# Gathered rows moved into earlier stages: four edits to a decoder block with a PEER layer

## The chip, the cores and the metric

The kernel runs on one core of one Trainium2 chip, as one launch. The metric is the device time of that launch in microseconds. Before the change it is 1765.07 us, the median of three runs (1763.4 to 1766.93).

## The reference, cut to what matters

One decoder block on 512 tokens of 1024 channels in float32. Two branches (retention and spatial gating) run on a normed input, are merged by gates and go through one output projection. Its result is scaled by a gate per channel and added to x:

```
x  = x + gate1 * (merged @ w_out)                    # residual
h2 = modulate(rms_norm(x, norm2_g), shift2, scale2)
q  = (h2 @ w_q) as (tokens, 8 heads, 2, 128);  s = q . sub_keys   # 128 scores per half
top 16 of each half;  cand = sub_s[0][:, None] + sub_s[1][None, :];  top 16 of the 256 sums
expert = k1 * 128 + k2                               # 16 of 16384 experts per head
act = gelu(h2 . expert_u[expert]) * softmax(top)     # 128 rows of 4 KB per token
x  = x + gate2 * sum(act * expert_v[expert]);  out = rms_norm(x, final_g)
```

So each token needs 128 rows of the table u and then 128 rows of the table v.

## The kernel before, in words

The 512 tokens are four tiles of 128. The last layer is done in two ways. For the first tile and the last one the rows are **gathered**: one indirect DMA from GpSimd's queue (line 934) brings one row for each of the 128 tokens, 0.524 MB, and one VectorE instruction takes it (`consume`): line 950 multiplies by h2 and sums to a dot, line 955 adds the row times its weight to `acc`. That is 4 x 128 = 512 gathers: u of the first tile (numbers 0 to 127), v of the first tile (128 to 255), then u and v of the last tile. For the two tiles between, all 16384 experts are computed as matmuls in 128 chunks, in a dense loop at the end (from line 1800): every chunk needs its v chunk, and its uT chunk has been done earlier (an `ahead` unit, plain f32, its result sent to `sd` and read back) or is done in the loop (`u_mm`, three passes).

The order is: modulation and the whole first tile (to some 290 us), including its lists of experts in four parts (`g_lists`, each raises `lim` by 32); 56 weight units for the other three tiles (`gemm`: w_in, w_sgu, w_ret); w_out, residual and second norm; query units; `ahead` units with lists and one-hots; the dense loop.

Weights come through a `Stream`: a unit of 512 KB lands in one of 5 `raw` buffers, ScalarE copies it to `wh` (line 87) and VectorE takes the rest `wl` (line 90), three units ahead of TensorE. A unit's optional `prep` runs on VectorE before that: the eight w_out units are multiplied by gate 1 there (line 344).

Gathers are set in program order. `gfree` is a list of free buffers, `gather_all` starts a gather for each while the number is under `lim`, `consume` takes the oldest and gives its buffer back. Behind each weight unit of the 56 `gemm` calls a hook, `bg_gather` (line 1017): it first works off one entry of `tq` (the first tile's remaining lists), then adds `GB1` to a credit (0.5 while `tq` is not empty) and takes as many rows as there is credit. Its buffers are two `ga`, one `gt` and one slot each of the rotating `wh` and `wl` tiles; before the two w_ret units two more `gt` are added, and after the first one `ga`, `wh` and `wl` are dropped. `lim` is 128 in this stage, and is set to 256 behind it (line 1230).

From the query units on, `plan` (line 103) writes the order out by hand. It keeps two clocks, P for TensorE and V for VectorE, and lets VectorE's steps in while V is at most P + 6. A credit pays for `gather` steps: `GPU` = 1.4 for each `ahead` unit, 1.0 for each query unit. What it holds up is drained behind the query units with more `ahead` units, so their number (NAH) comes out of it. What has not been gathered by then is spread evenly over the dense loop, on seven buffers.

The first tile's `acc0` lives in a pool opened behind the hooks (line 1228). `x2_tile` (line 1254) adds the w_out sums to x. Candidate sums of two lists are made by `stage2` on VectorE (lines 852 and 853), or earlier by `cands` on ScalarE (lines 840 and 841); the first tile uses the former.

Of the kernel before, what the change touches and what calls it, by code (L numbers as in the profile page):

```python
# [11 lines left out]
F32 = mybir.dt.float32  # L12
# [26 lines left out]
GPU = 1.4  # L39
GB1 = 2.2  # L40
VN = 2
# [61 lines left out]
def plan():  # L103
# [54 lines left out]
    for g in range(4):  # L158
        for u in range(4):
            if g and u:  # L160
                score(4 * (g - 1) + u)
            steps.append(("q", g, u))
            t["P"] += 4.2
            t["V"] += 1.15
            if t["go"]:
                t["credit"] += 1.0
            if g and not u:
                score(4 * (g - 1))
            pump()
# [21 lines left out]
def block_kernel(ctx: ExitStack, tc: tile.TileContext, a, out, dbg=None):  # L191
# [149 lines left out]
    for g in range(2):  # L341
        add_group(a["w_ret"], g)
    def gate_prep(r, g):
        V.tensor_tensor(r.rearrange("p (a n) -> p a n", a=2), r.rearrange("p (a n) -> p a n", a=2),
                        gates[:, 0:1, g * 512:(g + 1) * 512].to_broadcast([128, 2, 512]), op=OP.mult)
    add_two(a["w_out"], gate_prep)
    steps, NAH = plan()
# [630 lines left out]
    for g in range(4):  # L978
        units = []
        bks = [bank() for _ in range(4)]  # L980
        for u in range(4):
# [10 lines left out]
            if g and u == 2:  # L992
                st1_0(g - 1)
            if g == 2 and u == 3:
                stage2(l0, [(0, 0), (0, 1)])
# [8 lines left out]
        if g == 0:  # L1004
            h20_n()
    tq += [lambda: score0(3), lambda: st1_0(3), lambda: g_lists(l0, 0, GT[0], 1),
           lambda: stage2(l0, [(0, 4), (0, 5)]), lambda: g_lists(l0, 0, GT[0], 2),
           lambda: stage2(l0, [(0, 6), (0, 7)]), lambda: g_lists(l0, 0, GT[0], 3)]


    ga = [tmp.tile([128, 1024], F32, name="ga", tag="ada", bufs=4) for _ in range(2)]
    gfree += ga
    gfree.append(t0_tile("gt"))
    gfree += ["wh", "wl"]
    cr = [0.0]

# [194 lines left out]
    while any(dropped(b) for _, b in gt_t.values()):  # L1211
        consume()
        gather_all()
    bg[0] = lambda: None
    dump("mH", mH.bitcast(F32))
# [11 lines left out]
    h2F = hf.tile([128, ND, TA], F32, name="h2F")  # L1227
    GT[0].acc = kp.tile([128, D], F32, name="acc0")
    V.memset(GT[0].acc, 0.0)
    lim[0] = 2 * NJ  # L1230
    x2 = big([128, N3, D], F32, "x2")
# [8 lines left out]
    for u in range(4):  # L1240
        for g in range(2):
# [3 lines left out]
            if u < 2:  # L1245
                unit_mm("nat", u, w[0], w[1], mH, mL, [(bk[g][b], b) for b in range(N3)])
            else:
                last.append((u, g, w))
# [5 lines left out]
    def x2_tile(t):  # L1254
        for g in range(2):
            xx = x2[:, t, g * 512:(g + 1) * 512]
            V.tensor_tensor(xx, bk[g][t], xx, op=OP.add)
        P.dma_start(x2d[t + 1], x2[:, t, :])
# [655 lines left out]
```

## Time and profile before

| | us |
|---|---|
| median of three runs | 1765.07 |
| the profiled execution | 1765.71 |
| its span (first to last instruction) | 1763.7 |
| TensorE busy in it | 1589.2 (90%) |
| VectorE busy | 1414.4 (80%) |
| ScalarE busy | 581.4 (33%) |
| GpSimd busy | 750.5 (43%) |
| DMA, mean of the span | 341 GB/s, 601.82 MB |

PE is TensorE, PEld its weight loads, DVE is VectorE, ACT ScalarE, POOL GpSimd, SP the queue of plain loads. L955 is line 955 of the kernel. A row with `[1.20 <-DVE x L10]` says that the engine was idle for 1.20 us until line 10 on VectorE released it. "To landing" is the time from the issue of a DMA to its arrival. A gathered row of the first tile is named `E`, of the last one `EB`.

### The profile page before, as it was taken

To read this page: it belongs to the slowest core of one execution; us is meant where nothing else is said; L and a number is where in the kernel's file an instruction comes from. 1 tells how busy PE (TensorE), PEld (TensorE's weight loads), DVE (VectorE), ACT (ScalarE), POOL (GpSimd) and SP (SyncE) were. 2 spreads that over 40 slices of the span, in tenths; PEclk is the share of its full clock that TensorE was granted. 3 is DMA by queue.
4 is the path that set the end of the run, shared out by engine and by line. 5 is a ranking of instruction groups with operands and counts; after the bars stand their busy time and mean duration, and the time that the engine had idled before them with its cause. 6 is when DMAs were issued, how large, how long until landed. Compare 5 with 4: busy or idle time off the path is not lost.

```text
span 1763.7 us, 22139 instructions
## 1 busy us (share of the span) xinstructions
PE 1589.2 (90%) x7546; PEld 1237.1 (70%) x7546; DVE 1414.4 (80%) x2862; ACT 581.4 (33%) x914; POOL 750.5 (43%) x629
## 2 busy tenths in 40 slices
PE   9999999889999889999999998889888888888886
PEld 8544578789779768898888887556665656565553
DVE  7675356988789876999999994788878878888887
ACT  6322123332234234432136774242222222222222
POOL 0101001157447512146467653475545545555542
PEclk9999999989999889999999999899999999999998
DMA  8999857379879857479999999999999999999995
GB/s 334 381 353 377 320 193 261 124 270 373 287 246 351 307 187 280 156 258 410 387 391 375 389 390 366 373 407 409 408 408 408 408 408 408 408 408 406 408 405 207
DMA packets 168496, 601.82 MB, mean 341 GB/s; under 512 B 19072, under 2 KB 19072, under 8 KB 168256
## 3 DMA queue, kind: packets, MB, share of 16 engines
q0 software_dynamic: 87888, 320.64, 47.7%
q1 hardware_dynamic: 80496, 279.78, 42.1%
q8 instruction: 59, 0.97, 0.2%
q14 instruction: 53, 0.43, 0.1%
HBM read 568.89 MB, written 31.46 MB: 340 GB/s over the span
## 4 chain that ended last, share of the span: by engine, by line
DVE 25%; DMA 24%; PE 23%; issue 15%; POOL 9%; ACT 3%; SPq 0%; POOLq 0%; DVEq 0%; ACTq 0%
DMA gr<-in_v_dram,EB 10%; PE mm L416 6%; DVE acc L955 5%; POOL gr L934 4%; DMA gt<-in_v_dram,EB 3%; POOL gt L934 3%; DVE wl L90 3%; PE mm L384 2%; PE mm L385 2%; PE mm L383 2%; PE acc L1680 2%; DMA sd<-spl 1%; DMA gt<-in_v_dram,E 1%; DMA gwh<-in_u_dram,E 1%; DVE gt L950 1%
## 5 line engine op out<-in xcount | busy, mean ns | idle before, releaser
L90 DVE TENSOR_TENSOR wl<-raw,wh 128x1024 fp32r<-128x1024 f32 x208 | 259.0, 1249 | 68.2 <-ACT wh L87 66.1
L87 ACT CAST wh<-raw 128x1024 fp32r<-128x1024 f32 x208 | 216.8, 1048 | 255.6 <-DMA raw<-in_uT_dram 61.4
L1354 PE MATMUL mm<-h2F,raw 128*128 128x256 f32 (+1 forms) x1296 | 286.4, 382 | 0.6 <-ACT stg L1548 0.5
L1354 PEld LDWEIGHTS mm<-h2F,raw 128*128 128x128 f32 x1296 | 246.1, 193 | 34.5 <-ACT stg L1548 1.1
L1680 PE MATMUL acc<-raw,aw 128*128 128x512 f32 x512 | 235.9, 603 | 1.6 <-DVE aw L1653 1.6
L1680 PE MATMUL acc<-wh,ah 128*128 128x512 f32 x512 | 185.8, 465 | 48.8 <-DVE ah L1664 36.3
L1680 PEld LDWEIGHTS acc<-wh,ah 128*128 128x128 f32 x512 | 103.0, 208 | 98.8 <-DVE ah L1664 43.7
L1680 PEld LDWEIGHTS acc<-raw,aw 128*128 128x128 f32 x512 | 97.9, 195 | 99.6 <-issue 92.4
L1661 ACT CAST ah<-aw 128x256 fp32r<-128x256 f32 x64 | 26.1, 407 | 341.4 <-DVE aw L1653 341.4
L934 POOL DMA_INDIRECT gr<-in_v_dram,EB x74 | 94.2, 1273 | 82.6 <-DVE accB L955 69.5
L934 POOL DMA_INDIRECT ga<-in_u_dram,E x44 | 65.7, 1493 | 132.4 <-DVE ga L950 75.2
L1344 PE MATMUL mm<-h2H,wh 128*128 128x256 f32 x384 | 119.0, 310 | 1.4 <-ACT wh L87 1.4
L1680 PE MATMUL acc<-wl,ah 128*128 128x512 f32 x256 | 91.9, 442 | 31.5 <-DVE wl L90 31.5
L1346 PE MATMUL mm<-h2H,wl 128*128 128x256 f32 x384 | 111.6, 291 | 7.2 <-DVE wl L90 7.1
L955 DVE SCALAR_TENSOR_TENSOR accB<-gr,dB,accB 128x1024 f32<-128x1024 f32 x74 | 94.9, 1282 | 25.3 <-DMA gr<-in_v_dram,EB 24.4
L934 POOL DMA_INDIRECT gr<-in_u_dram,EB x72 | 84.7, 1176 | 69.5 <-DVE gr L950 58.3
L1345 PE MATMUL mm<-h2L,wh 128*128 128x256 f32 x384 | 110.5, 288 | 0.0
L934 POOL DMA_INDIRECT gt<-in_v_dram,E x46 | 63.2, 1374 | 108.8 <-DVE acc L955 51.2
L416 PE MATMUL mm<-raw,h 128*128 128x512 f32 x224 | 101.9, 598 | 3.4 <-DMA raw<-in_w_in_dram 3.3
L950 DVE SCALAR_TENSOR_TENSOR gr<-gr,h2B 128x1024 f32<-128x1024 f32 x72 | 86.9, 1221 | 22.0 <-DMA gr<-in_u_dram,EB 22.0
L934 POOL DMA_INDIRECT gt<-in_u_dram,EB x56 | 69.3, 1238 | 65.7 <-DVE gt L950 53.5
L934 POOL DMA_INDIRECT gt<-in_v_dram,EB x54 | 65.2, 1208 | 56.5 <-DVE accB L955 40.1
(448 smaller groups left out, 3713.1 us busy)
## 6 DMA issues: line engine op xcount, KB each, us to landing
raw<-in_uT_dram SPq DMA_DIRECT2D x128, 512.0 KB, 7.2
raw<-in_v_dram SPq DMA_DIRECT2D x128, 512.0 KB, 10.5
raw<-in_w_in_dram SPq DMA_DIRECT2D x112, 512.0 KB, 6.5
raw<-in_w_q_dram SPq DMA_DIRECT2D x32, 512.0 KB, 4.6
wd<-stg POOLq DMA_DIRECT2D x8, 2048.0 KB, 17.1
wqb<-wd SPq DMA_DIRECT2D x32, 512.0 KB, 12.7
ada<-in_w_ada_dram POOLq DMA_DIRECT2D x28, 512.0 KB, 7.4
sd<-spl POOLq DMA_DIRECT2D x40, 256.0 KB, 8.6
```

The lines of the kernel that those rows point to most:

```text
L87: self.nc.scalar.copy(h, r)
L90: self.nc.vector.tensor_tensor(l, r, h.bitcast(F32), op=OP.subtract)
L383: T.matmul(ps, sH[:, d, ab], wH[:, dd, :], start=st, stop=False)
L416: T.matmul(ps, s[:, d, :], r[:, dd * 512:(dd + 1) * 512], start=(d == 0), stop=(d == ND - 1))
L934: P.indirect_dma_start(out=r, out_offset=None, in_=a[tab], in_offset=bass.IndirectOffsetOnAxis(ap=G.E[:, j:j + 1], axis=0))
L950: V.scalar_tensor_tensor(r, r, 1.0, G.h, op0=OP.mult, op1=OP.mult, accum_out=G.dots[:, j:j + 1])
L955: V.scalar_tensor_tensor(G.acc, r, G.dots[:, j:j + 1], G.acc, op0=OP.mult, op1=OP.add)
L1344: T.matmul(ps[:, p:q], h[:, d, :], h2H[:, d, cs], start=(d == 0), stop=False)
L1345: T.matmul(ps[:, p:q], h[:, d, :], h2L[:, d, cs], start=False, stop=False)
L1346: T.matmul(ps[:, p:q], l[:, d, :], h2H[:, d, cs], start=False, stop=(d == ND - 1))
L1354: T.matmul(ps[:, p:q], r[:, d, :], h2F[:, d, p:q], start=(d == 0), stop=(d == ND - 1))
L1680: T.matmul(accs[2 * t + e], s_, y[:, e * 512:(e + 1) * 512], start=s0_, stop=s1_)
```

## The change

The residual's gate no longer multiplies the eight w_out units; it multiplies the sums in `x2_tile`, with `xn2` as scratch. `acc0` becomes a tile of the pool t0, in the place of the gather buffer `gt`, and is cleared before the hooks; in its old place a gather buffer `gk` is added to the list behind the hooks. A new last entry of `tq` sets `lim` to 256, so rows of v may follow those of u in the hooks. The hooks go on behind the first four w_out units. `GB1` goes from 2.2 to 2.5, and the credit of a query unit from 1 to 2. The first tile's candidate sums are made by `cands`.

```diff
-GB1 = 2.2
+GB1 = 2.5
...
             if t["go"]:
-                t["credit"] += 1.0
+                t["credit"] += 2.0
...
-    def gate_prep(r, g):
-        V.tensor_tensor(r.rearrange("p (a n) -> p a n", a=2), r.rearrange("p (a n) -> p a n", a=2),
-                        gates[:, 0:1, g * 512:(g + 1) * 512].to_broadcast([128, 2, 512]), op=OP.mult)
-    add_two(a["w_out"], gate_prep)
+    add_two(a["w_out"])
...
+            if g and u == 3:
+                cands(l0, [(0, 2 * g - 2), (0, 2 * g - 1)])
...
-    tq += [lambda: score0(3), lambda: st1_0(3), lambda: g_lists(l0, 0, GT[0], 1),
+    tq += [lambda: score0(3), lambda: (st1_0(3), cands(l0, [(0, 6), (0, 7)])), lambda: g_lists(l0, 0, GT[0], 1),
...
+    def all_0():
+        lim[0] = 2 * NJ
+    tq.append(all_0)
...
-    gfree.append(t0_tile("gt"))
     gfree += ["wh", "wl"]
+    GT[0].acc = t0_tile("acc0")
+    V.memset(GT[0].acc, 0.0)
...
-    bg[0] = lambda: None
...
-    GT[0].acc = kp.tile([128, D], F32, name="acc0")
-    V.memset(GT[0].acc, 0.0)
-    lim[0] = 2 * NJ
+    gfree.append(kp.tile([128, D], F32, name="gk"))
...
                 unit_mm("nat", u, w[0], w[1], mH, mL, [(bk[g][b], b) for b in range(N3)])
+                bg[0]()
...
-            V.tensor_tensor(xx, bk[g][t], xx, op=OP.add)
+            w = xn2[:, t, g * 512:(g + 1) * 512]
+            V.tensor_tensor(w, bk[g][t], gates[:, 0, g * 512:(g + 1) * 512], op=OP.mult)
+            V.tensor_tensor(xx, xx, w, op=OP.add)
```

## Rows read from the trace of the kernel before

**Rows 1.** by stretch: us, busy PE, PEld, DVE, ACT, POOL; clock, DMA share, GB/s.

```profile
395.00:437.00 42.00, 40.97 (x224) 38.68 (x224) 38.72 (x61) 10.15 (x11) 30.11 (x22) 1.00 1.00 379
516.00:594.00 78.00, 73.38 (x399) 69.30 (x400) 70.57 (x106) 25.74 (x35) 57.06 (x39) 0.98 0.96 355
594.00:634.00 40.00, 24.41 (x101) 20.50 (x99) 34.54 (x54) 9.64 (x14) 11.66 (x11) 0.77 0.67 227
634.00:677.00 43.00, 39.38 (x186) 32.17 (x186) 28.64 (x56) 22.37 (x40) 6.27 (x9) 0.90 0.49 167
677.00:780.00 103.00, 98.42 (x550) 95.22 (x550) 88.82 (x355) 42.87 (x90) 26.60 (x25) 0.95 0.69 234
780.00:1083.00 303.00, 292.11 (x1699) 256.40 (x1698) 286.00 (x629) 139.88 (x207) 178.96 (x148) 0.98 1.00 383
1083.00:1745.00 662.00, 572.92 (x2408) 393.72 (x2408) 535.93 (x709) 162.44 (x237) 347.12 (x280) 0.94 1.01 400
```

**Rows 2.** DMA of 1083 to 1745, in 40 slices.

```profile
GB/s 350 383 365 385 409 405 411 408 408 410 407 408 407 409 407 408 408 409 407 409 407 409 408 409 408 409 406 409 408 407 408 408 408 402 409 408 408 400 408 240
```

**Rows 3.** busy us and count on L950 (two records each), by stretch.

```profile
292.00:614.00 322.00, 129.27 (x216) 0.93 0.78 281
```

**Rows 4.** the same view for L955.

```profile
677.00:1083.00 406.00, 145.12 (x113) 0.97 0.92 345
```

**Rows 5.** chain of waits from 677 to 1083, shares by line.

```profile
by line: DVE acc L955 21.0%; issue 9.2%; DMA sd<-spl 6.1%; DMA gt<-in_v_dram,E 6.0%; DMA gwh<-in_v_dram,E 3.7%; PE mm L1354 3.4%; DVE wk L821 2.8%; DVE MI L819 2.8%; DVE ohA L1528 2.8%; DMA raw<-in_uT_dram 2.6%; DVE ohB L1529 2.5%; DVE MI L
```

**Rows 6.** L90 by stretch: busy us of VectorE and count.

```profile
395.00:437.00 42.00, 10.99 (x9) 1.00 1.00 379
516.00:594.00 78.00, 20.22 (x17) 0.98 0.96 355
```

**Rows 7.** DMA issues from 380 to 410: count, median us to landing.

```profile
ga<-in_u_dram,E POOLq DMA_INDIRECT x6, 7.3
```

**Rows 8.** DMA issues from 515 to 550.

```profile
gt<-in_u_dram,E POOLq DMA_INDIRECT x3, 5.7
```

**Rows 9.** DMA issues from 600 to 625.

```profile
gt<-in_u_dram,E POOLq DMA_INDIRECT x5, 4.9
```

**Rows 10.** timeline of GpSimd near 525.

```profile
525.59 1.68 POOL L934 DMA_INDIRECT ga<-in_u_dram,E  x1 [0.60 <-DVE ga L950]
```

**Rows 11.** timeline of VectorE from 575 to 680.

```profile
605.10 1.22 DVE L950 SCALAR_TENSOR_TENSOR gt<-gt,h 128x1024 f32<-128x1024 f32 x1
622.22 0.08 DVE L950 DVE_READ_ACCUMULATOR gt<-gt,h 128x1 f32 x1
630.54 0.56 DVE L1202 TENSOR_TENSOR mL<-mg,mH 128x384 fp32r<-128x384 f32 x1 [0.58 <-ACT mH L1201]
631.27 0.91 DVE L1229 MEMSET acc<- 128x1024 f32 x1 [0.16 <-issue]
646.32 1.23 DVE L90 TENSOR_TENSOR wl<-raw,wh 128x1024 fp32r<-128x1024 f32 x1 [2.85 <-ACT wh L87]
650.63 0.69 DVE L1257 TENSOR_TENSOR x<-mm,x 128x512 f32<-128x512 f32 x1 [0.67 <-PE mm L385]
```

**Rows 12.** instructions of L344: ns min/median/max, first and last start.

```profile
L344 DVE TENSOR_TENSOR raw<-raw,gates x8: 1162/1221/1223, 607.4 to 641.1; 128x1024 f32<-128x1024 f32 x8
```

**Rows 13.** instructions of L1257.

```profile
L1257 DVE TENSOR_TENSOR x<-mm,x x6: 682/688/692, 649.3 to 666.9; 128x512 f32<-128x512 f32 x6
```

**Rows 14.** timeline of VectorE near 303.

```profile
302.92 0.23 DVE L852 TENSOR_SCALAR cand<-MV 128x16 f32<-128x16 f32 x1
303.06 0.23 DVE L853 TENSOR_SCALAR cand<-MV 128x8 f32<-128x8 f32 x1
```

**Rows 15.** instructions of L841.

```profile
L841 ACT ACTIVATE cand<-MV x16: 286/288/288, 711.4 to 891.3; 128x8 f32<-128x8 f32 x16
```

**Rows 16.** timeline of TensorE near 1301.

```profile
1301.38 0.68 PE L1344 MATMUL mm<-h2H,wh 128*128 128x256 f32 x1
1304.62 0.63 PE L1680 MATMUL acc<-wh,ah 128*128 128x512 f32 x2
```

## The prediction

> **What bounds the kernel now.** I read busy time by stretch first [rows 1], then the DMA by slice, then the chain of waits, then single instructions where the change cuts in. The reader is to see four stages. From 292 to 614 us come the 56 weight units (I call the call behind each a hook) of the second to fourth token tiles: TensorE is busy 41 of 42 and 73 of 78 us in two stretches [rows 1], while VectorE takes gathered rows behind it (L950). From 614 to 677 come w_out, the residual and the second norm; TensorE is idle 15.6 us between 594 and 634, where the eviction of the last w_ret unit is late. From 677 to 1083 come queries, lists and `ahead` units: VectorE is busy 375 of 406 us, its gather step L955 leads the chain of waits with 21% [rows 5], and from 780 the DMA is full too, 383 GB/s at a share of 1.00. From 1083 to 1745 comes the dense loop: DMA flat at 408 GB/s [rows 2], TensorE 573 of 662 us. So a gathered row (128 x 4 KB = 0.524 MB) costs 1.28 us in the dense loop because it is bytes, and 1.28 us between 677 and 1083 because it is a VectorE instruction (145.12 us for 113 [rows 4]). Only where both have room is it cheap.
>
> **Counts, walked through the code.** The credits, the free list and `plan()` are plain arithmetic, so they can be followed row by row. Before: 113 rows are taken by the end of the hooks, 113 by the end of w_out, 233 by the end of `plan`'s steps, and 271 are left for the dense loop (the trace agrees on the 113 that L955 takes before 1083 [rows 4], 128 + 113 = 241 in all). After: 126, 136, 284, and 219 left. The second credit per query unit also pushes list work later, so `plan` emits 88 `ahead` units, not 80; 40 full uT units are left for the dense loop, not 48. Of the second table only 8 rows are taken before the queries. The price hides in the free list: acc0 takes the t0 tile that was the gather buffer `gt`. Four buffers, not five, turn during the hooks; two during the last w_ret unit, where there were three; three during w_out.
>
> **Dense loop.** 52 rows and 8 units less are 31.5 MB; four more `sd` pairs to read add 1.05 MB. 30.4 MB at 408 GB/s [rows 2]: **-74.5 us**. Could TensorE take over? A full uT unit takes it 3.2 us (1301.38 to 1304.62 [rows 16]), so 8 less leave 573 - 26 = 547 us busy in some 588: it fits, barely. If its 89 idle us all stayed, only the 26 would be won; so the ends are -80 and -26. The flat DMA rows are the nearest, so I take -74.5.
>
> **Queries and ahead.** 148 gather steps for 120: 28 more at 1.28 us on the engine that leads the chain: **+36 us**. The DMA side asks 36 x 0.524 MB plus four `sd` writes, 19.9 MB: 50 us if no idle time takes it, 20 us if the 32 idle us of 677 to 780 (share 0.69, 234 GB/s [rows 1]) take 12.2 MB first. Range +20 to +50. The rows beside the query units themselves cost little there, because `plan` moves two stage-1 sets, one list and one stage-2 set of the last tile behind them.
>
> **The hooks.** 26 of them are TensorE-bound (9 + 17 splits [rows 6]) and take 42 + 78 = 120 us, 4.62 us each. A buffer's turn is 0.60 us until GpSimd starts after the consumer [rows 10], the landing, and 1.20 us of L950 (129.27 us for 108 [rows 3]). Landing is 7.3 us around 390 [rows 7] and 5.7 us around 530 [rows 8]. Four buffers at 2.5 rows a hook thus need (0.60 + 7.3 + 1.20) x 2.5 / 4 = 5.69 us a hook, or 4.69 with 5.7 us. Five at 2.2, with 7.3 us, needed 4.0: the ring did not bind before. Over 26 hooks that is +28 or +2 us. The load would be 3.5 x 0.524 MB in some 5.1 us, 357 GB/s, as between 516 and 594; I take 6.4 us of landing, 5.13 us a hook: **+13** (+2 to +28). In the other hooks five more rows at 1.20 us lie on a VectorE that is partly idle: **+2** (0 to +6).
>
> **Last w_ret unit.** Before, VectorE's hooks run from 605.10 to 622.30, 17.2 us without a gap [rows 11], three gate multiplies of 1.22 us among them [rows 12]. After: ten rows and four splits at 1.20 us, 16.8 us. But rows 124 and 125 go into the two buffers that rows 122 and 123 have just left. With 0.60 + 4.9 us [rows 9] after each and one split between, VectorE waits 3.1 and 1.2 us. The eviction that TensorE's w_out waits for stands behind them in the queue: **+4** (0 to +8).
>
> **w_out.** What goes: the memset (0.91 us) and one gate multiply ahead of the split that TensorE waits for; the other four were hidden, since the splits end at 647.5 and TensorE sets 650.6 [rows 11]. What comes: four hooks, ten rows, three buffers. One turn is 0.60 + 4.9 + 1.20 = 6.7 us; ten rows are three turns and one, 21.3 us. The last split (1.2 us) is queued behind them, then 1.4 us of matmul, and row 128 needs the Gelu of all 128 dots, a round trip to ScalarE, some 1.5 us: 25.4 us from the end of the eviction to the first tile's sum. Before it was 650.6 - 631.1 = 19.5. That is +6; with 7.3 us of landing it is +13; if no row makes VectorE wait, -2. I take **+7**.
>
> **Residual.** The gate now multiplies the sums: six 128x512 reads of PSUM (0.69 us [rows 13]) and six adds in SBUF, no row for these, bounded by 0.5 and 0.69. Two of three tiles lie on the path: **+2** (+1 to +4). **Candidate sums.** Sixteen instructions leave VectorE, 0.14 us apart [rows 14]; 0.29 us each on ScalarE [rows 15], where the query copies stand behind them and wait for stage 1: **-1** (-2 to +3).
>
> **Sum.** -1 + 13 + 2 + 4 + 7 + 2 = +27 us up to the queries, +36 to the dense loop, -74.5 in it: -11.5. The profiled execution took 1765.7 us (span 1763.7), 0.6 us above the median of 1765.07. So 1754.2, and I say 1754.
>
> **A rule against the trace.** The landings above are 4.9 to 7.3 us for 0.524 MB, longer with more load [rows 7 to 9]. The Trainium skill, page "DMA: Bandwidth & Descriptors", section "Anatomy of one DMA — SWDGE (gpsimd) path", fits a DMA from GpSimd as about 2.0 us plus its bytes at 436 GB/s, an estimate of 3.2 us here. By it a turn is 5.0 us, four buffers need 3.1 us a hook, and the lost buffer is free: the first rival below. The trace does not agree: its shortest median is 4.9 us, in a light stretch, and this estimate enters no term.
>
> **Rivals.** (1) *The ring never binds.* Hooks +2 + 2, last unit 0, w_out -2, residual +2, lists -1: +3, then +36 - 74.5: **1730**. For it: VectorE may run up to three units ahead of TensorE, and each eviction lets the ring refill. Against: at 7.3 us of landing four buffers need 5.69 us a hook, and TensorE 4.62. 14%. (2) *The ring binds everywhere* (slower). Place: the line `gfree.append(t0_tile("gt"))` that goes. Price: +28 + 2 + 8 + 13 + 2 - 1 = +52, +36 - 74.5 = +13.5: **1779**. It decides from +38.5 us before the queries on, which is a landing of some 6.8 us. For it: 7.3 us near 390; and a gather into wh or wl also waits for a weight tile's last matmul. 18%. (3) *TensorE takes over the dense loop* and the gain stops at about 50 us, halfway between the two ends: -11.5 + 24.5, **1779**. For it: 547 us busy of 588. Against: the flat DMA. 8%. (4) *Moved, not removed:* the rows do start earlier, but the DMA, full from 780 on, takes 50 us and not 36: **1768**, which no measurement tells from no change. For it: share 1.00 in 780 to 1083. Against: the idle DMA of 677 to 780. 12%.
>
> **Numbers.** The forecast holds 48%, its own range 1743 to 1761. About 0.2%, 3.5 us, is what a measurement of this kernel can tell from no change. Faster: 48 + 14 = 62%. Same: 12%. Slower: 18 + 8 = 26%. The range of 8 in 10 goes from 1733 to 1778, short of the ends of rivals 1 and 2.
>
> **What the profile after would show.** Dense loop: 219 rows, 40 uT units, about 588 us, DMA still 408. From the queries to the dense loop 436 to 446 us. Hooks in the sgu and ga stretches at 5 us and more, with `DVE ga L950 <- DMA` among the waits; near 4.6 us the ring was no bound. Between the eviction and the first tile's sum some 25 us, with VectorE idle for `gt` and `gk`. I am wrong if the stages before the queries grow by over 38 us, or if the dense loop shrinks by under 55.

## The result and the profile after

The changed kernel takes 1779.23 us (median of 5, 1775.86 to 1782.2) against 1765.07 us: ratio 1.0084, 95% interval 1.0059 to 1.0109 (from all runs, not from the two medians). It is slower; the forecast of 1754 us was wrong, with the sign. Its profiled execution has a span of 1777.5 us (before: 1763.7).

First the busy time by stretch of the changed kernel, columns as in [rows 1]; the bounds follow the same places of the code, which now come later.

```profile
395.00:437.00 42.00, 34.16 (x184) 32.88 (x182) 31.25 (x47) 8.07 (x10) 24.45 (x19) 0.96 0.93 335
516.00:594.00 78.00, 65.50 (x324) 59.70 (x323) 66.41 (x111) 28.70 (x40) 48.42 (x33) 0.91 0.88 306
594.00:640.00 46.00, 34.10 (x167) 32.63 (x166) 37.51 (x59) 9.08 (x11) 25.48 (x18) 0.85 0.85 305
640.00:690.00 50.00, 32.00 (x103) 23.85 (x101) 32.67 (x42) 9.51 (x12) 19.74 (x18) 0.80 0.77 264
690.00:725.00 35.00, 29.34 (x143) 23.64 (x142) 24.75 (x52) 20.18 (x38) 6.95 (x10) 0.85 0.54 195
725.00:813.00 88.00, 82.26 (x483) 81.35 (x482) 80.31 (x211) 31.85 (x67) 40.27 (x32) 0.96 0.78 276
813.00:1167.00 354.00, 329.16 (x1882) 288.55 (x1880) 325.31 (x822) 149.57 (x232) 205.49 (x171) 0.98 0.98 377
1167.00:1745.00 578.00, 531.89 (x2198) 360.44 (x2199) 453.98 (x602) 150.31 (x215) 291.08 (x228) 0.96 1.02 403
```

In 395 to 437 TensorE falls from 41.0 of 42 us to 34.2, and the DMA from 379 to 335 GB/s [rows 1]: neither is full any more, so both wait for something else. From 516 to 594 it is the same (73.4 to 65.5, 355 to 306). From 813 on DMA, TensorE and VectorE are about as full as before. The granted clock falls too where TensorE waits (0.91 for 0.98 from 516 to 594); how much of the loss that makes, no run parts from the waits.

The stage lengths come from the first starts of TensorE's matmuls (line, operation, count, ns min/median/max, first to last start): hH, the first hook; zH, w_ret; yH, the eight sgu units among the hooks; the 128 of h2H, the queries; the 320 of h2H, the dense loop. Here is the changed kernel.

```profile
L385 PE MATMUL mm<-hH,wh x192: 333/334/689, 290.1 to 589.6; 128*128 128x384 f32 x192
...
L385 PE MATMUL mm<-zH,wh x64: 334/334/687, 590.1 to 640.3; 128*128 128x384 f32 x64
...
L385 PE MATMUL mm<-yH,wh x64: 334/334/522, 392.8 to 436.1; 128*128 128x384 f32 x64
...
L385 PE MATMUL mm<-h2H,wh x128: 334/337/527, 725.3 to 810.0; 128*128 128x384 f32 x128
...
L1348 PE MATMUL mm<-h2H,wh x320: 274/282/687, 1167.3 to 1722.4; 128*128 128x256 f32 x160
```

The sgu units take 43.3 us from first to last start, where the same matmuls took 33.6 before (396.2 to 429.8). Most of that is not the missing buffer's: with five buffers at 2.5 rows a hook they still take 40.4 (e1) and 39.4 (e12). The first w_out matmul (mH) is at 640.8. Read in the same way from each trace, the stages are (us, the last one to the end of the span):

```
kernel                          first tile  hooks  w_ret  w_out+resid.  queries+ahead  dense   span
before                             293.2    277.0   44.8      67.2          401.1      680.4  1763.7
changed                            290.1    300.0   50.7      84.5          442.0      610.2  1777.5
e1  five buffers again             288.3    286.4   48.8      83.3          445.9      610.0  1762.7
e5  e1, no hooks in w_out          291.2    289.7   49.6      68.7          443.1      622.4  1764.7
e10 changed, six buffers late      290.6    294.0   49.3      84.8          442.4      609.9  1771.0
e2  changed, 2.2 rows a hook       289.9    280.0   47.6      80.3          444.2      629.3  1771.3
e3  before, four buffers           288.8    285.3   49.2      67.1          401.4      680.2  1772.0
e12 before, 2.5 rows a hook        291.2    286.4   49.2      70.0          405.5      666.6  1768.9
e13 before, 1.9 rows a hook        292.2    264.2   40.4      64.4          400.7      701.7  1763.6
e17 before, narrow rows in hooks   291.6    256.2   41.7      61.0          401.5      682.0  1734.0
e15 e12, narrow rows in hooks      290.2    262.3   45.7      63.9          404.4      663.5  1730.0
e16 e3, narrow rows in hooks       293.8    266.8   44.5      61.1          401.3      681.8  1749.3
e4  before, second credit          290.9    277.7   43.1      66.8          446.0      638.6  1763.1
e8  e4, narrow second-table rows   289.7    276.4   47.5      67.4          420.7      638.0  1739.7
e6  before, gate on sums           291.7    279.1   41.2      64.2          401.8      679.8  1757.8
e7  before, sums on ScalarE        290.0    272.9   44.3      65.0          400.4      681.4  1754.0
e9  e6 + e7                        287.9    273.7   44.1      64.1          402.4      680.5  1752.7
e11 e9, seven buffers late          290.5    269.7   45.0      69.5          401.5      680.2  1756.4
e14 e9, 1.9 rows a hook            290.4    262.8   40.4      63.7          400.0      702.5  1759.8
```

The changed kernel loses 43.1 us ahead of the queries (725.3 for 682.2) and 40.9 in queries and ahead, and wins 70.2 in the dense loop: +13.8. There is one profile of each kernel. Ten of them (before, e3, e4, e6, e8, e12, e13, e15, e16, e17) have the same first tile and take 288.8 to 293.8 us for it; three (before, e4, e8) have the same code up to w_out and take 276.4 to 277.7 in the hooks and 43.1 to 47.5 in w_ret. So a single stage scatters by some 4 us, the hooks by less, and only larger differences, or those that several kernels repeat, are read.

The hooks once more, parted at the first start of the first sgu unit and of the eleventh unit from their end (before: 396.2 and 513.4; us):

```
kernel                          16 units  21 units  last 11
before                            103.0     117.2     56.8
e4, same code up to here          101.0     119.8     56.9
e8, same code up to here          100.7     118.6     57.0
changed                           102.7     129.9     67.4
e1  five buffers again            102.5     124.8     59.1
e10 changed, six buffers late      99.9     133.4     60.7
e12 before, 2.5 rows a hook       101.9     125.6     58.9
e17 before, narrow rows            93.6     112.3     50.4
e15 e12, narrow rows               94.1     120.0     48.2
```

The missing buffer (changed against e1) costs 8.3 us in the last eleven hooks and 5.1 in the 21 ahead of them; the higher rate alone (e12 against before) costs 8.4 in those 21.

What TensorE waits for in the hooks and w_ret (290 to 640), in the changed kernel (engine, line <- what ended the wait: us in total, times, longest):

```profile
PE mm L387 <- DVE wl L90: 28.8, 14, 5.1
```

And what VectorE waits for there:

```profile
DVE ga L947 <- DMA ga<-in_u_dram,E: 28.4, 20, 4.5
DVE gwl L947 <- DMA gwl<-in_u_dram,E: 9.3, 4, 3.0
DVE gwh L947 <- DMA gwh<-in_u_dram,E: 4.4, 6, 1.4
```

Before, the same two views have

```profile
PE mm L390 <- DVE wl L90: 7.9, 6, 3.4
```

```profile
DVE ga L950 <- DMA ga<-in_u_dram,E: 5.9, 8, 1.7
```

and 5.9 (gwl), 1.4 (gwh) and 0.9 us (gt) for the other gathered rows. TensorE's 20.9 us more are nearly the 23.0 by which the hooks grew (the second matmul line that waits for wl has 7.2 us, and 8.1 before). How the one wait makes the other is seen on VectorE's timeline (start, duration, idle time before it in brackets):

```profile
408.00 1.22 DVE L947 SCALAR_TENSOR_TENSOR ga<-ga,h 128x1024 f32<-128x1024 f32 x1
...
411.34 1.23 DVE L947 SCALAR_TENSOR_TENSOR ga<-ga,h 128x1024 f32<-128x1024 f32 x1 [2.12 <-DMA ga<-in_u_dram,E]
...
412.66 1.23 DVE L947 SCALAR_TENSOR_TENSOR gwh<-gwh,h 128x1024 f32<-128x1024 f32 x1
...
413.81 1.22 DVE L90 TENSOR_TENSOR wl<-raw,wh 128x1024 fp32r<-128x1024 f32 x1
```

The second row waits 2.12 us for its landing; the weight split (L90) is queued two instructions behind it, and TensorE needs that split. VectorE starts these rows in the order of the program, so here a row that lands late is a weight that is split late.

In w_out, the same view, from the last eviction to the first residual:

```profile
657.84 0.56 DVE L1206 TENSOR_TENSOR mL<-mg,mH 128x384 fp32r<-128x384 f32 x1 [0.58 <-ACT mH L1205]
...
670.54 1.28 DVE L952 SCALAR_TENSOR_TENSOR acc<-gt,d,acc 128x1024 f32<-128x1024 f32 x1 [2.77 <-DMA gt<-in_v_dram,E]
671.74 1.22 DVE L90 TENSOR_TENSOR wl<-raw,wh 128x1024 fp32r<-128x1024 f32 x1
...
682.66 1.28 DVE L952 SCALAR_TENSOR_TENSOR acc<-gt,d,acc 128x1024 f32<-128x1024 f32 x1 [1.26 <-DMA gt<-in_v_dram,E]
683.86 2.35 DVE L90 TENSOR_TENSOR wl<-raw,wh 128x1024 fp32r<-128x1024 f32 x2
687.68 0.69 DVE L1260 TENSOR_TENSOR xn<-mm,gates 128x512 f32<-128x512 f32 x1 [1.46 <-PE mm L382]
```

From the end of the eviction, 658.4, to the first sum, 687.7, it is 29.3 us; the forecast said 25.4. Before, it was 18.2: the first sum starts at 649.3 [rows 13], 18.2 us after the eviction's end at 631.1; the forecast's 19.5 runs to the second sum, at 650.6 [rows 11].

The dense loop is as flat as before, at the same 408 GB/s in nearly all slices [rows 2]:

```profile
GB/s 293 407 367 388 406 409 408 407 407 408 408 409 408 406 409 407 408 407 409 404 409 409 408 408 409 402 409 407 405 408 408 407 407 409 407 409 409 393 408 402
```

### The profile page after: what moved, and what is told of

It is laid out like the page before. It is cut to its first block, busy times and chain, and to the rows that moved or that the text cites. A ratio compares the mean times of both kernels' runs of the same rounds, so it can differ in the third digit from the quotient of the medians.

```text
span 1777.5 us, 21980 instructions
## 1 busy us (share of the span) xinstructions
PE 1594.0 (90%) x7482; PEld 1236.7 (70%) x7482; DVE 1400.1 (79%) x2836; ACT 577.4 (32%) x923; POOL 764.1 (43%) x633
## 4 chain that ended last, share of the span: by engine, by line
DVE 22%; PE 20%; DMA 19%; issue 8%; POOL 3%; ACT 2%; DVEq 0%; POOLq 0%; ACTq 0%; SPq 0%
PE acc L1684 11%; DMA raw<-in_v_dram 11%; DVE acc L952 6%; DMA sd<-spl 2%; DMA raw<-in_uT_dram 1%; DVE accB L952 1%; DVE wl L90 1%; PE mm L1358 1%; ACT wh L87 1%; DMA gt<-in_u_dram,EB 1%; PE mm L1348 1%; PE mm L1349 1%; PE mm L1350 1%; DMA gt<-in_v_dram,E 1%; DMA ga<-in_u_dram,E 1%
## 5 line engine op out<-in xcount | busy, mean ns | idle before, releaser
L90 DVE TENSOR_TENSOR wl<-raw,wh 128x1024 fp32r<-128x1024 f32 x200 | 244.1, 1223 | 130.1 <-ACT wh L87 125.0
L1358 PE MATMUL mm<-h2F,raw 128*128 128x256 f32 (+1 forms) x1424 | 312.1, 380 | 1.0 <-ACT stg L1552 0.9
L1358 PEld LDWEIGHTS mm<-h2F,raw 128*128 128x128 f32 x1424 | 269.1, 192 | 37.7 <-ACT stg L1552 1.8
L931 POOL DMA_INDIRECT ga<-in_u_dram,E x60 | 89.2, 1487 | 167.5 <-DVE ga L947 104.6
L1348 PE MATMUL mm<-h2H,wh 128*128 128x256 f32 x320 | 99.2, 310 | 13.1 <-ACT wh L87 13.1
L1350 PE MATMUL mm<-h2H,wl 128*128 128x256 f32 x320 | 93.2, 291 | 2.4 <-DVE wl L90 2.4
L947 DVE SCALAR_TENSOR_TENSOR ga<-ga,h 128x1024 f32<-128x1024 f32 x60 | 72.4, 1220 | 28.7 <-DMA ga<-in_u_dram,E 28.4
L1349 PE MATMUL mm<-h2L,wh 128*128 128x256 f32 x320 | 92.9, 290 | 0.0
L931 POOL DMA_INDIRECT gr<-in_u_dram,EB x52 | 65.6, 1261 | 58.1 <-DVE gr L947 49.8
L387 PE MATMUL mm<-hH,wl 128*128 128x384 f32 x192 | 69.7, 363 | 18.0 <-DVE wl L90 18.0
L381 PE MATMUL mm<-wl,hH 128*128 128x512 f32 x192 | 76.9, 400 | 7.8 <-DVE wl L90 7.8
```

The lines of the kernel that those rows point to most:

```text
L90: self.nc.vector.tensor_tensor(l, r, h.bitcast(F32), op=OP.subtract)
L381: T.matmul(ps, sH[:, d, ab], wL[:, dd, :], start=False, stop=False)
L931: P.indirect_dma_start(out=r, out_offset=None, in_=a[tab], in_offset=bass.IndirectOffsetOnAxis(ap=G.E[:, j:j + 1], axis=0))
L947: V.scalar_tensor_tensor(r, r, 1.0, G.h, op0=OP.mult, op1=OP.mult, accum_out=G.dots[:, j:j + 1])
L1348: T.matmul(ps[:, p:q], h[:, d, :], h2H[:, d, cs], start=(d == 0), stop=False)
L1349: T.matmul(ps[:, p:q], h[:, d, :], h2L[:, d, cs], start=False, stop=False)
```

## The experiments

Ratios are to the kernel before, measured beside each on the same chip.

**e1: the fifth buffer back.**

```diff
+    gfree.append(t0_tile("gt"))
-    GT[0].acc = t0_tile("acc0"); V.memset(GT[0].acc, 0.0)
-    gfree.append(kp.tile([128, D], F32, name="gk"))
+    GT[0].acc = kp.tile([128, D], F32, name="acc0"); V.memset(GT[0].acc, 0.0)
```

> The changed kernel with one thing undone: the fifth gather buffer `gt` turns in the hooks' ring again, and acc0 lies where it lay before. The rate of 2.5 rows a hook, the hooks behind the w_out units, the gate on the sums, the candidate sums and the second credit stay. Theory A (the ring): the hooks grew by 23 us because four buffers wait for landings. Five at 2.5 need (0.60 + 7.3 + 1.20) x 2.5 / 5 = 4.55 us a hook, TensorE needs 4.62: the stretch from the first hook to the first w_ret unit goes back from 300 to about 280 us, VectorE's waits for ga, gwl and gwh in it from 42 to under 20 us, the last w_ret unit loses some 4 us (three buffers, not two), w_out keeps its 12 us (three buffers, as in the changed kernel): about 1755 us. Theory B (the rows): 13 rows more on VectorE and the transfers beside the weights are what costs; the hooks stay at 295 to 300 us, total 1774 to 1780.

Measured: 1763.73 us, 1.0003 (0.9988 to 1.0017). The whole loss goes with this one edit. It is not theory A's 1755, though: the hooks are 13.6 us shorter than in the changed kernel, but stay 9.4 us longer than before, and TensorE still waits 21.4 us for wl. So theory A holds for 14 us, and a second price is left.

```profile
PE mm L387 <- DVE wl L90: 21.4, 16, 4.1
```

**e3: four buffers alone.**

```diff
-    gfree.append(t0_tile("gt"))
-    gfree += [t0_tile("gt") for _ in range(2)]     # at w_ret
+    gfree += [t0_tile("gt") for _ in range(3)]
```

> The kernel before with one thing of the change alone: `gt` joins the ring only at the w_ret units, so that the hooks turn four buffers, still at 2.2 rows a hook. Every count of rows is that of before. Theory A: four at 2.2 need 9.1 x 2.2 / 4 = 5.0 us a hook with a landing of 7.3 us, 4.4 with 6 us, against TensorE's 4.62: the stretch from the first hook to w_ret grows by 4 to 12 us, total 1769 to 1777 us, VectorE's waits for ga, gwl and gwh from 14 to over 25 us. Theory B (it is the rate of 2.5 and not the buffer): within 3 us of before, 1762 to 1768.

Measured: 1.0078 (1.0059 to 1.0096), 13.8 us, with no row more and none earlier: theory A, a little over its total. Hooks and w_ret grow by 8.3 and 4.4 us. The waits, TensorE's and then VectorE's:

```profile
PE mm L390 <- DVE wl L90: 18.3, 10, 4.2
```

```profile
DVE ga L950 <- DMA ga<-in_u_dram,E: 17.6, 16, 3.1
DVE gwh L950 <- DMA gwh<-in_u_dram,E: 10.6, 9, 2.7
...
DVE gwl L950 <- DMA gwl<-in_u_dram,E: 4.7, 4, 2.3
```

**e10: two buffers earlier in the changed kernel.** The line that gives the ring its two late tiles stands ahead of the second half of the g units.

```diff
+    gfree += [t0_tile("gt") for _ in range(2)]
     gemm("nat", hH, hL, ev_g(1))
-    gfree += [t0_tile("gt") for _ in range(2)]     # at w_ret
```

> The changed kernel with one line moved: the two `gt` tiles that join the ring with the w_ret units join two stages earlier, ahead of the second half of the g units (what held their room, v0 and qk0, has its last reader by then). So the ring has six buffers, not four, in the last 4 g and 8 ga units and the first 4 w_ret units, and four up to there. Rows taken are the same. Ring theory: VectorE's waits for gathers, 10.6 us between 536 and 590 and 5.1 us between 590 and 614 in the changed kernel, go from that part, the part up to 442 us keeps its growth: 8 to 12 us less, 1767 to 1771. If the DMA itself is the bound there (share 0.90 to 0.95) and not the buffers: 1776 to 1780.

Measured: 1.0052 (1.0038 to 1.0066), against 1.0084: some 5.6 us of the loss come back, 6.0 in the hooks; less than the 8 to 12 expected. It comes where the ring theory has it: the last eleven hooks, behind the moved line, fall from 67.4 to 60.7 us, near e1's 59.1, and the part ahead of it is 0.7 longer. So more buffers win back there 6.7 of the 8.3 us that the missing one costs.

**e12: the rate alone.** `GB1 = 2.5` in the kernel before.

> The kernel before at 2.5 rows a hook, with its five buffers, and nothing else of the change: 126 rows before w_out, not 113, and 13 fewer in the dense loop, which gives back 13 x 1.28 = 17 us. By the forecast's terms the ring of five does not bind (4.55 us a hook at a landing of 7.3 us, against 4.62) and the 13 rows cost the hooks some 2 us: 1765 - 15 = 1750, faster. By the two kernels with five buffers at 2.5 (hooks 286 and 290 us for 277, last w_ret unit 49 for 45) they cost 13 to 17 us: 1761 to 1765, nothing gained.

Measured: 1.0043 (1.0028 to 1.0058), slower even than the second theory. Thirteen rows cost 9.4 us in the hooks, 4.4 in w_ret, 2.8 in w_out and 4.4 behind it, 21 in all, and give back 13.8 in the dense loop. So with five buffers the rows have a price of their own; in the hooks it falls between the first sgu unit and the last eleven (8.4 of the 9.4 us). From 395 to 437 the DMA is full, and TensorE has lost 2.3 us to before:

```profile
395.00:437.00 42.00, 38.67 (x205) 37.00 (x205) 37.33 (x58) 10.02 (x11) 31.35 (x23) 0.96 0.99 373
516.00:594.00 78.00, 68.75 (x357) 63.13 (x355) 70.54 (x111) 29.30 (x40) 52.25 (x38) 0.96 0.93 343
```

```profile
PE mm L390 <- DVE wl L90: 17.4, 16, 3.4
```

**e13: a lower rate.** `GB1 = 1.9` in the kernel before.

> The kernel before at 1.9 rows a hook, five buffers, nothing else: 97 rows before w_out, not 113, and 16 more in the dense loop, 20 us. Between 2.2 and 2.5 each of 13 rows cost the stages ahead some 1.6 us and gave back 1.1 to 1.3. If a row has that price at any rate, 16 rows fewer give 26 us for 20: 1755 to 1760, faster than before. If the price sets in only where the DMA is full (share 1.00 and 379 GB/s at 2.2 rows already, but TensorE hardly waits: 7.9 us for weight splits, against 17.4 at 2.5), the rows below 2.2 were nearly free and the dense loop's 20 us stay: 1773 to 1783, and 2.2 is the optimum.

Measured: 0.9992 (0.9978 to 1.0005): neither theory. Sixteen rows fewer give 12.8 us in the hooks, 4.4 in w_ret and 2.8 in w_out, 20.0, and cost 21.3 in the dense loop. So, by one profile each, a row costs about 1.25 us ahead of the dense loop between 1.9 and 2.2 rows a hook, about what it saves later (1.33), and 1.6 between 2.2 and 2.5, where it saves 1.06. It is nowhere nearly free, and that is not read from the stretch 395 to 437, where TensorE and the DMA look at 1.9 as they do at 2.2 [rows 1]; VectorE does not (33.0 of 42 us for 38.7):

```profile
395.00:437.00 42.00, 41.11 (x220) 38.47 (x220) 32.98 (x51) 8.33 (x8) 23.87 (x19) 1.00 1.00 380
```

**e17, e15, e16: what the price is made of.** The kernel before (e17), e12 (e15) and e3 (e16); in each, the rows that the hooks take enter the dot product with 128 of 1024 columns.

```diff
-            V.scalar_tensor_tensor(r, r, 1.0, G.h, ...)
+            c = slice(0, thin[0])                  # 128, then D from w_out on
+            V.scalar_tensor_tensor(r[:, c], r[:, c], 1.0, G.h[:, c], ...)
```

> The kernel before; of each first-table row that the hooks take only the first 128 of 1024 columns go into the dot product (this leaves out part of it). 113 rows at some 0.35 us for 1.22: about 98 us less on VectorE ahead of w_out, every transfer as it was. Theory V (VectorE's instruction is the price of a row there: it is busy 92 of 103 us from 290 to 393 and 38.7 of 42 from 395 to 437): hooks and w_ret, 277 and 45 us, fall to 255 and 40 or less, the total by 25 us and more. Theory D (the full DMA and the landings are the price): the hooks stay above 270, the total falls by less than 8 us.

> The same narrow rows at 2.5 rows a hook with five buffers. With whole rows, the step from 2.2 to 2.5 makes the hooks 9.4 us longer and the whole 7.6 us slower. Theory V: with VectorE out of the way the 13 rows are nearly free in the hooks (within 3 us of the narrow kernel at 2.2), and the total is 10 to 15 us below it. Theory D: the hooks are still 7 to 10 us longer than in the narrow kernel at 2.2, and the total is the same or higher.

> The same narrow rows at 2.2 with four buffers in the hooks. With whole rows, the fourth buffer for the fifth costs 13.8 us. A turn of a buffer is 0.60 + 7.3 + 0.35 us here: four need 4.54 us a hook at 2.2 rows, TensorE 4.62. Theory V (late rows cost because VectorE has no room to catch up): the loss against the narrow kernel with five buffers goes to under 5 us. If a late landing stops the weight split whatever VectorE has to do, it stays at 8 us and more.

Measured: 1732.34 us (0.9818, 0.9796 to 0.984), 1732.67 us (0.9822, 0.9798 to 0.9845) and 1751.29 us (0.9922, 0.9891 to 0.9953).

e17 is theory V: with VectorE's instruction cut, hooks, w_ret and w_out are 20.8, 3.1 and 6.2 us shorter, 30 in all, at the same transfers (the figures for hooks and w_ret, 255 and 40, are missed by 1.2 and 1.7 us). At 2.2 rows a hook VectorE bounds these stages by 30 us; that the last rows' 1.25 us each are all VectorE's would take narrow rows at 1.9, and there is no such run.

e15 is not: against e17 its 13 rows still cost 6.1 us in the hooks, 4.0 in w_ret, 2.9 in w_out and 2.9 behind it, 16 in all, and save 18.5; the totals are the same. In the hooks the price falls between the first sgu unit and the last eleven, as with whole rows (7.7 us for 8.4). The sgu units, in e17 and then in e15:

```profile
385.20:417.90 32.70, 32.70 (x190) 32.70 (x189) 16.09 (x48) 8.81 (x9) 20.91 (x18) 1.00 1.03 408
```

```profile
384.30:422.60 38.30, 33.88 (x191) 32.62 (x191) 17.19 (x54) 8.68 (x9) 23.74 (x21) 1.00 1.01 391
```

The DMA is full in both, VectorE half idle, and TensorE waits in e15 alone. e15 moves 15.0 MB there and e17 13.3; at 408 GB/s the difference is 4.0 of the 5.6 us. So most of the step to 2.5 is paid to the DMA there. The ring is not parted from it: with e15's landings of 7.7 to 9.0 us from 395 to 437 five buffers need some (0.60 + 8.3 + 0.35) x 2.5 / 5 = 4.6 us a hook, where a sgu unit takes 4.1, and no run has more than five buffers there.

e16 shows that the ring's price does not hang on VectorE's load: the fourth buffer for the fifth costs 19 us with narrow rows, 13.8 with whole ones. The turn expected, 4.54 us a hook, took a landing of 7.3 us, which e16's gathers have from 395 to 437. From 536 to 590 they land later (count, median us); with 8.9 us four buffers need (0.60 + 8.9 + 0.35) x 2.2 / 4 = 5.4 us a hook for TensorE's 4.62.

```profile
ga<-in_u_dram,E POOLq DMA_INDIRECT x11, 8.9
gwl<-in_u_dram,E POOLq DMA_INDIRECT x6, 9.5
gt<-in_u_dram,E POOLq DMA_INDIRECT x6, 10.5
```

**e2: the changed kernel at 2.2.**

> The changed kernel at 2.2 rows a hook, as before the change, with its four buffers; 111 rows come before w_out, not 126, and 235 are left to the dense loop, not 219. Ring theory: four buffers at 2.2 cost the hooks 8 us, as the kernel before with four buffers alone shows, not 23; the dense loop takes 16 rows x 1.28 = 20 us back: 1779 - 15 - 2 + 20 = about 1782, and no gain from the lower rate. If the rate of 2.5 was the fault and four buffers are enough at 2.2, the hooks are as before the change, 1779 - 23 + 20 = 1776 or less, as w_out has a row less too.

Measured: 1.0046 (1.0029 to 1.0063), below both figures. Hooks of 280.0 us, 20.0 less for 15 rows less, and the dense loop 19.1 more; the rest is w_ret and w_out, 7.3 less. Four buffers do bind at 2.5 more than at 2.2, as the ring has it (13.6 us by e1, 8.3 by e3); that the total would not fall was wrong.

**e5: no hooks in w_out.** e1 without the call behind the four units.

```diff
                 unit_mm("nat", u, w[0], w[1], mH, mL, ...)
-                bg[0]()
```

> As the kernel with the fifth buffer back, and without the hooks behind the four w_out units: their ten rows are left to the dense loop. Theory A (three buffers in w_out make the last split late): w_out goes back from 47 to about 35 us, and ten rows more in the dense loop cost 10 x 1.28 = 13 us, so the same total as with the hooks, about 1755 us. Theory C (VectorE was idle enough in w_out and its 12 us come from something else, the order of the queue at the last eviction): w_out stays at 45 us and more, total 1765 to 1770.

Measured: 1.0009 (0.9997 to 1.002), as e1. Ten rows cost w_out and the residual 14.6 us (83.3 for 68.7), 13.3 of them in w_out, and are worth 12.4 in the dense loop. That the two come out alike is what theory A expected (its 1755 is missed by both, for the rows in the hooks).

**e4: the second credit alone.** `t["credit"] += 2.0` in the kernel before.

> The kernel before with the second credit per query unit alone: 29 rows and 8 uT units less are left to the dense loop (242 rows, 40 units), and none is taken earlier than the queries. If the rows beside the queries cost what the changed kernel shows, queries and ahead grow by 41 us, and the dense loop shrinks by (29 + 8) x 0.524 MB less 1.05 MB, 18.3 MB at 408 GB/s, 45 us: total 1757 to 1763 us. If they are only moved (the DMA pays for 28 rows, 8 units and four writes of sd, 50 us), 1766 to 1772. If VectorE's 1.28 us a row is all that they cost, 36 - 45, 1756.

Measured: 0.9999 (0.9989 to 1.001). Queries and ahead +44.9, dense loop -41.8: moved, not removed. On the 1765 us that the cases were worked out from, that lies between the first two.

**e8: who pays there.** In e4, each second-table row taken before the dense loop accumulates 128 of its 1024 columns.

```diff
-            V.scalar_tensor_tensor(G.acc, r, G.dots[:, j:j + 1], G.acc, ...)
+            c = slice(0, thin[0])                  # 128, then D in the dense loop
+            V.scalar_tensor_tensor(G.acc[:, c], r[:, c], G.dots[:, j:j + 1], G.acc[:, c], ...)
```

> The kernel before with the second credit, and of each second-table row that is taken before the dense loop only the first 128 of 1024 columns are accumulated (this leaves out part of the gathered sum): 128 rows at some 0.25 us for 1.28, about 130 us less on VectorE, with every transfer as it was. With the second credit alone, queries and ahead take 446 us. Theory D (the DMA pays for rows there, and TensorE is close behind): from 810 us on the DMA is at a share of 0.98 to 1.00, so the stage stays above 430 us. Theory V (VectorE pays, 1.28 us a row, as the forecast has it): the stage falls until DMA and TensorE stop it, 290 us busy of 310, to 415 to 425 us, and the total by 20 to 30 us.

Measured: 0.9867 (0.9843 to 0.9891). The stage falls by 25.3 us to 420.7, as theory V has it. Busy time by stretch, first of e4, then of e8, and e8's chain of waits:

```profile
678.00:765.00 87.00, 79.65 (x458) 78.08 (x457) 77.66 (x205) 30.62 (x63) 37.58 (x31) 0.96 0.79 281
765.00:1124.00 359.00, 334.55 (x1906) 293.92 (x1904) 330.30 (x819) 151.53 (x238) 205.99 (x173) 0.98 0.98 374
```

```profile
681.00:756.00 75.00, 75.00 (x454) 74.97 (x453) 59.26 (x206) 30.52 (x62) 35.22 (x32) 1.00 0.87 321
756.00:1102.00 346.00, 329.31 (x1909) 291.32 (x1908) 230.75 (x817) 154.49 (x239) 176.64 (x172) 0.99 1.00 387
```

```profile
by line: PE mm L1357 51.0%; DMA wd<-stg 8.7%; DMA sd<-spl 8.3%; issue 5.7%; PE mm L390 5.4%; PE mm L389 5.4%; PE mm L388 5.3%; DMA gt<-in_u_dram,EB 4.1%; PE mm L1389 2.5%; PE mm L1550 0.6%; PE mm L1549 0.6%; DVE ohA L1531 0.6%; DVE ohB L153
```

VectorE does 118 us less and the stage is 25 shorter (a narrow row takes 0.35 us, not 0.25): then TensorE is busy 75 of 75 and 329 of 346 us, the DMA is at 1.00, and TensorE's L1357 leads the chain with 51%. VectorE is the bound there, by 25 us of 446; TensorE and the DMA come next.

**e6, e7, e9: the edits without rows.** e6: the gate on the sums, without the eight gate multiplies on the weights ([rows 12]; the text of e6 counts six). e7: the candidate sums on ScalarE. e9: both.

```diff
-    add_two(a["w_out"], gate_prep)
+    add_two(a["w_out"])                                         # e6
...
-            V.tensor_tensor(xx, bk[g][t], xx, op=OP.add)
+            V.tensor_tensor(w, bk[g][t], gates[...], op=OP.mult)     # e6
+            V.tensor_tensor(xx, xx, w, op=OP.add)
...
+            if g and u == 3: cands(l0, ...)                          # e7
...
```

> The kernel before with one edit of the change alone: the residual multiplies the gate onto the sums out of PSUM and adds them in SBUF, and the six gate multiplies on w_out's weights go. Taken by the forecast's terms: 1 to 4 us on the residual, less one gate multiply of 1.22 us ahead of the last split: 1764 to 1768 us. If the multiplies were late in the last w_ret unit and in w_out (six times 1.22 us on the engine whose split TensorE waits for), the last unit and w_out shrink by 3 to 7 us against a residual 4.7 us longer, as the changed kernel had it: 1760 to 1765.

> The kernel before with one edit of the change alone: the first tile's candidate sums on ScalarE. The first tile was 3.1 us shorter in the changed kernel, but the other kernels, with and without this edit, have between 288.3 and 291.2 us there, so I expect nothing that shows: 1762 to 1767. If the 3 us are the edit's, 1760 to 1763.

> Both of the two edits of the change that touch no gathered row: the gate on the sums and the candidate sums on ScalarE, in the kernel before. If the two effects add and the first is worth 2 to 4 us, 1758 to 1763 us, faster than both kernels; if neither is worth anything, 1763 to 1767.

Measured: 1.0000 (0.9987 to 1.0013), 1.0000 (0.9988 to 1.0012) and 0.9990 (0.9975 to 1.0005). None shows by itself. In the profiles the two kernels with the candidate sums have hooks of 272.9 and 273.7 us for 277.0, and w_out with the residual is 2 to 3 us shorter in all three, with the gate on the sums and without: within the scatter (e7's profile is its fastest run, 1756.8 us for a median of 1763.0).

**e11: seven buffers late.** e9 with e10's line.

> The kernel before with the gate on the sums, the candidate sums on ScalarE, and the two late `gt` tiles joining ahead of the second half of the g units: seven buffers there, not five. The kernel before waits 6 us for gathers between 536 and 590, with the DMA at 0.96 to 1.02. If those waits are the ring's, 3 to 5 us less than the two edits alone (1760): 1755 to 1758, faster than both kernels. If they are the DMA's, as its share says, nothing: 1759 to 1762.

Measured: 0.9992 (0.9982 to 1.0002), as e9. At 2.2 rows more than five buffers win nothing that can be measured.

**e14: a faster version.** e9 at 1.9 rows a hook.

> The same rate of 1.9 with the gate on the sums and the candidate sums on ScalarE, which with 2.2 gave 0.999 of before. A row that costs the same at any rate: 1752 to 1757. A price that sets in with the full DMA: 1770 to 1780.

Measured: 1757.39 us, 0.9966 (0.9951 to 0.9981): faster than both kernels. The first case expected a slightly larger gain, the second is out. The rate alone (e13, 0.9992) and the two edits alone (e9, 0.9990) don't show by themselves; together they do. Whether they give more together than their sum stays open: the intervals allow both.

## Why the prediction was wrong

By its own terms, forecast and measured (us; the pairs of starts as above, all of w_ret for its last unit, w_out and residual parted at the first residual operation, 649.3 before and 687.7 after):

```
lists -1 / -3.1     hooks +15 / +23.0     last w_ret unit +4 / +5.9     w_out +7 / +12.6
residual +2 / +4.7  queries and ahead +36 / +40.9   dense loop -74.5 / -70.2   sum -11.5 / +13.8
```

**Every count was right**: 219 rows and 40 units are left to the dense loop (320 matmuls of h2H), and it is at 408 GB/s. Six terms of seven fell short on the same side, and one of them by its idea, not its size. The forecast's own sign of being wrong, over 38 us ahead of the queries, came: 43.1.

**The ring was priced right.** The forecast gave the lost buffer +13 us in the hooks; the changed kernel against e1 gives 13.6. The line it named, `gfree.append(t0_tile("gt"))`, is the one that makes the change slow (e1, e3). That the sizes meet is partly luck: the +13 is counted from hooks that lose nothing with five buffers, and those of e1 lose 9.4 us.

**The step that failed** is that the 26 dense hooks are priced by the ring alone: "Five at 2.2, with 7.3 us, needed 4.0: the ring did not bind before", with 4.62 us a hook as the floor at any rate. The eight of the 13 more rows that fall there get no price of their own; the only term for rows is +2, for five of them in the other hooks. With five buffers the 13 rows cost 9.4 us in the hooks and 21 in all (e12), and 8.4 of the 9.4 fall in the part with the sgu units. Two rows spoke against it, and both stood in the forecast. VectorE was busy 38.7 of 42 and 70.6 of 78 us in those stretches [rows 1], so its 1.2 us a row had little room: e13's 1.25 us a row and e17's 30 us agree with that up to 2.2 rows a hook. And the DMA carried 379 GB/s at a share of 1.00 there [rows 1], while 3.5 transfers of 0.524 MB in TensorE's 4.62 us ask 397; the forecast got 357 because it had already stretched the hook to 5.13 us. From 2.2 to 2.5 that is most of the price, as it stays with VectorE's instruction cut (e15); what five buffers add to it there is open.

**Landing.** The turn of a buffer was worked out with 5.7 us from 515 to 550 [rows 8], three issues at the lighter end of a stretch that gets full. From 536 to 590 the gathers of the kernel before land so (count, median us):

```profile
ga<-in_u_dram,E POOLq DMA_INDIRECT x9, 8.2
gt<-in_u_dram,E POOLq DMA_INDIRECT x7, 9.3
```

and gwh and gwl in 8.6 and 7.8. With 8.5 us four buffers at 2.5 need (0.60 + 8.5 + 1.20) x 2.5 / 4 = 6.4 us a hook, and five 5.2. In e12, whose hooks are longer, it is

```profile
ga<-in_u_dram,E POOLq DMA_INDIRECT x11, 6.9
...
gwl<-in_u_dram,E POOLq DMA_INDIRECT x5, 8.2
```

With 7.5 us, between these, five buffers at 2.5 need (0.60 + 7.5 + 1.20) x 2.5 / 5 = 4.65 us a hook: even five are then at their end.

**w_out, residual and w_ret.** The ten rows in w_out were priced at +7 by their turns in three buffers, +9 without the memset and the multiply that go. They cost 13.3 us in w_out (45.5 in e1 for 32.2 in e5) and 1.3 in the residual. The Gelu's round trip, 1.5 us in that sum, is shown by no row of before; in the changed kernel VectorE is past it 0.7 us after the last dot (662.30 to 662.97). From the first residual operation to the first query matmul it is 32.4 to 33.3 us with the gate on the weights (before, e3, e4, e7, e8, e12, e13, e17), 35.5 to 36.5 with it on the sums (e5, e6, e9, e11, e14), and 37.4 to 37.8 with rows in w_out as well (changed, e1, e2, e10). So the edit itself lengthens the residual by some 3 us, inside the +1 to +4 given (its multiplies and adds are 0.68 and 0.69 us), and the rows do the rest of the 4.7. In w_out the edit gives at least as much back: 28.7 and 28.6 us in e6 and e9, for 34.2 to 34.4 in before, e3, e4 and e8 (e11, with 33.1, does not show it). That fits e6, which as a whole is no slower. In w_ret the changed kernel has 50.7 us and those at 2.5 with five buffers 48.8 to 49.6 (e1, e5, e12): the buffer's part there is within the scatter.

**Queries and ahead.** +36 was VectorE's 28 x 1.28 us; it came to 40.9, and 44.9 for e4. e8 shows the reason to be right (VectorE bounds the stage), with TensorE and the DMA close behind; what makes it 41 to 45 and not 36 is not shown. The total of rival 4 is what the second credit gives by itself, but not its cause: rival 4 put the price to the DMA, and e8 takes 25 us off with every transfer as it was.

**Rival 2** gave 1779, the time that came, from 38.5 us on ahead of the queries; they came 43.1 later. Its place is confirmed, its price only in sum, and by luck: of its +52 ahead of the queries 43.1 came, and queries and dense loop came 9.2 us worse than its figures. It put 28 us of the hooks to the ring, and of the 23 that came 13.6 were the ring's. The rule of the Trainium skill, page "DMA: Bandwidth & Descriptors", section "Anatomy of one DMA — SWDGE (gpsimd) path", gave an estimate of 3.2 us a landing and with it a free buffer. The runs do not agree: landings of 6.9 to 8.2 us (e12), and 13.8 us for the buffer (e3).

## What to carry to other kernels

Before work is moved forward, price it on every engine of the stretch it goes to: TensorE bound the hooks, but where it was busiest VectorE was 92% busy and the DMA full (395 to 437), and a row cost there what it saved elsewhere. Count a ring's buffers by the landing under the load that the change itself makes, and look for what is queued behind the consumer: here a landing 2 us late was a weight split late. Where bytes only move between nearly full stages, the side edit (the buffer given up for it) decides the sign.

## What the runs showed of the hardware

An indirect gather of 0.524 MB lands in 4.9 us in a light stretch [rows 9] and in 8.9 to 10.5 us (medians by buffer) in e16 from 536 to 590, some twice as long at the same size. The same VectorE accumulation takes 1.28 us for 1024 columns [rows 4] and 0.35 us for 128 (e8), over a quarter of the time for an eighth of the columns:

```profile
L958 DVE SCALAR_TENSOR_TENSOR acc<-gt,d,acc x48: 331/351/356, 709.0 to 1030.2; 128x128 f32<-128x128 f32 x48
```
